# A masked softmax: the last 16 partitions of one batch stored through GpSimd's queue, and nine small reads after the last store

## The chip, the cores and the metric

The kernel runs on one core of a Trainium2 chip. That core has compute engines that run side by side, each with its own instruction stream: TensorE, VectorE, ScalarE, GpSimd and SyncE (here SyncE only issues transfers and waits). Sixteen DMA engines move data between the chip's memory (HBM) and the core's on-chip memory (SBUF), which has 128 partitions. A transfer issued by SyncE or ScalarE goes through a hardware queue of that engine; one issued by GpSimd goes through GpSimd's software queue. All queues are worked off by the same sixteen DMA engines. Order between the streams is kept with semaphores: a transfer adds to its semaphore when its data has landed (16 for a whole transfer), and an engine can wait until a semaphore has reached a number.

The metric is the device time of one launch in microseconds (us), as the median of several runs.

## The reference

The input `x` has the shape 16 x 8 x 256 x 256 (batch, heads, query, key) in float32, and every batch has one length between 128 and 255. For each row the softmax is taken over the first `length` keys; the rest of the row is zero.

```python
for b in range(batch):
    length = lengths[b]
    masked = x[b, :, :, :length].copy()
    masked = masked - np.max(masked, axis=-1, keepdims=True)
    exp_masked = np.exp(masked)
    result[b, :, :, :length] = exp_masked / np.sum(exp_masked, axis=-1, keepdims=True)
```

33.55 MB of output have to be written. Of the input, only the columns up to the length of the batch have to be read.

## The kernel before

One batch has 2,048 rows of 256 values. They lie on 128 partitions with 16 rows each (`nt` = 16, `half` = 8, `quarter` = 4), so one batch takes 16 KB of each partition, 2 MB in all. The tile `xt` has eight slots of one batch each; batch b is loaded into slot b % 8, changed in place, and stored from there.

**Loads.** SyncE issues the loads of batches 0 to 3 at full width (lines 107 to 111). From batch 4 on, GpSimd issues them in a loop (lines 153 to 160): it reads the length, waits until the store that freed the slot has landed, and picks one of twelve widths (160, 168, ... 240, 256 columns), so that it reads little more than is needed. The columns from 160 on of slots 4 to 7 have been set to zero before (line 149).

**Compute.** For each batch VectorE first pushes all columns past the length to a very negative number (`mask`, line 204, with `clip`, line 192). ScalarE then takes the exponential row by row and the sum of each row with it (lines 246 to 254, one semaphore count of `s_exp` per half batch). VectorE takes the reciprocal of the sums and multiplies (`divide`, line 216); each half batch adds one to `s_out`. The loop of lines 231 to 240 places the mask of the next batch among the two divides of this one; for batch 14 the mask of batch 15 comes first, then the two divides of 14, then the two of 15.

**Stores.** SyncE's stream, after its five load issues, is a plain list of stores (lines 114 to 122). `parts(b)` cuts a batch: batch 0 and batch 13 are stored whole, batches 1 to 7 in a half and two quarters, the others in two halves. Each store waits for its count of `s_out` (line 117); the first one of a batch also waits until the stores of the batch two before have landed (line 119, semaphores `s_st[0]` and `s_st[1]` for even and odd batches). Every store covers all 128 partitions:

```python
nc.sync.dma_start(
    out=out_f[b, :, s, :], in_=xt[:, b % slots, s, :]
).then_inc(s_b, 16 * ((s.stop - s.start) // quarter))
```

The order of the transfers in a queue is thus the order of the issues in the program. At the end SyncE waits until the stores of batches 14 and 15 have landed (lines 257 to 259), and the program closes.

Of the kernel before, what the change touches and what calls it, by code (L numbers as in the profile page):

```python
# [9 lines left out]
F32 = mybir.dt.float32  # L10
# [10 lines left out]
def kernel(  # L21
# [6 lines left out]
    nc = tc.nc  # L28
    P = nc.NUM_PARTITIONS

    batch, heads, seq_q, seq_k = x.shape
# [3 lines left out]
    half = nt // 2  # L35
    quarter = nt // 4

    x_f = x.rearrange("b h q k -> b (h q) k").rearrange("b (p t) k -> b p t k", p=P)
    out_f = out.rearrange("b h q k -> b (h q) k").rearrange("b (p t) k -> b p t k", p=P)

    slots = 8
# [2 lines left out]

    widths = list(range(160, 248, 8))
    low = widths[0]
    mid = seq_k // 2
    big = 1.0e30

    def parts(b):  # L50


        if b == 0:
            cuts = [0, nt]
        elif b < 8:
            cuts = [0, half, half + quarter, nt]
        elif b != batch - 3:
            cuts = [0, half, nt]
        else:
            cuts = [0, nt]  # L60
        return [slice(i, j) for i, j in zip(cuts, cuts[1:])]

    pool = ctx.enter_context(tc.tile_pool(name="all", bufs=1))
    psum = ctx.enter_context(tc.tile_pool(name="psum", bufs=1, space=bass.MemoryType.PSUM))
    xt = pool.tile([P, slots, nt, seq_k], F32, name="xt")
# [9 lines left out]
    inv_sum = pool.tile([P, batch, nt], F32, name="inv_sum")  # L75
    warm = pool.tile([P, 1], F32, name="warm")
    seed = pool.tile([1, 2], F32, name="seed")

    sem = lambda n: ctx.enter_context(nc.semaphore(n))
    s_st = [sem("s_st0"), sem("s_st1")]  # L80
    with tc.tile_critical(no_gpsimd_drain=True):  # L81
        s_word = sem("s_word")
        s_ones = sem("s_ones")
# [11 lines left out]
        s_out = sem("s_out")  # L95

        def length(engine, at):

            return nc.values_load(  # L99
                at,  # L100
                engines=[engine],
                skip_runtime_bounds_check_because="compared with constants, never an address",
            )


        nc.scalar.dma_start(out=word64, in_=lengths[None, :]).then_inc(s_word, 16)
        for h in range(2):
            s = slice(h * half, (h + 1) * half)
# [5 lines left out]
        for b in range(batch):  # L114
            s_b = s_st[b % 2]
            for s in parts(b):
                nc.sync.wait_ge(s_out, 2 * b + (s.stop - 1) // half + 1)
                if b >= 2 and s.start == 0:
                    nc.sync.wait_ge(s_b, 64 * (b // 2 + 1))
                nc.sync.dma_start(  # L120
                    out=out_f[b, :, s, :], in_=xt[:, b % slots, s, :]
                ).then_inc(s_b, 16 * ((s.stop - s.start) // quarter))

        def pick(v, n, slot, par, ws):

            if len(ws) == 1:
                w = ws[0]
                nc.gpsimd.dma_start(  # L130
                    out=xt[:, slot, :, :w], in_=x_n[:, n, :, :w]
                ).then_inc(s_sw[par], 16)
                return
            m = (len(ws) - 1) // 2
            with nc.gpsimd.If(v <= ws[m]):  # L135
                pick(v, n, slot, par, ws[: m + 1])
            with nc.gpsimd.Else():  # L137
                pick(v, n, slot, par, ws[m + 1 :])
# [14 lines left out]
        with nc.Fori(0, (batch - ahead) // 2, 1, engines=[POOL]) as q:  # L153
            for par in range(2):
                n = 2 * q + (ahead + par)
                v_len = length(POOL, word[0:1, bass.ds(2 * n, 1)])
                with nc.gpsimd.If(q >= 1):  # L157
                    nc.gpsimd.wait_ge(s_sw[par], 16 * q)
                    nc.gpsimd.wait_ge(s_st[par], 64 * q)  # L159
                pick(v_len, bass.ds(n, 1), bass.ds(n % slots, 1), par, widths + [seq_k])  # L160


        nc.tensor.wait_ge(s_ones, 1)
# [6 lines left out]
        def step(ins):  # L170
# [8 lines left out]
                out=down, in0=iota_i, scalar1=0.5, scalar2=-big, op0=ALU.add, op1=ALU.mult  # L179
# [7 lines left out]
                out=len_s, in0=len_f, scalar1=big, scalar2=None, op0=ALU.mult  # L187
# [58 lines left out]
        with nc.Fori(0, 2 * batch, 1, engines=[ACT]) as i:  # L246
            nc.scalar.wait_ge(s_min, i + 1)
            at = bass.ds(i % (2 * slots), 1)
            for j in range(half):
                e = x_h[:, at, j, :]  # L250
                ins = nc.scalar.activation(  # L251
                    out=e, in_=e, func=EXP, accum_out=sum_h[:, bass.ds(i, 1), j]
# [4 lines left out]
    with tc.tile_critical(no_gpsimd_drain=True):  # L257
        for par in range(2):
            nc.sync.wait_ge(s_st[par], 64 * (batch // 2 + 1))


# [28 lines left out]
```

The softmax here doesn't subtract the row's maximum and nothing guards it: scores larger than these inputs give would overflow.

## Time and profile before

| what | value |
|---|---|
| median of 9 runs | 156.3 us (155.81 to 156.71) |
| the profiled execution, its own time | 156.24 us |
| its span in the profile | 154.6 us |
| bytes moved | 62.08 MB (28.51 MB read from HBM, 33.55 MB written), 401 GB/s over the span |
| VectorE busy | 115.6 us, 75% of the span |
| ScalarE busy | 105.2 us, 68% |
| GpSimd busy | 19.0 us, 12% |
| VectorE's multiply on half a batch (line 222) | 32 times, 2292 ns each |
| GpSimd's issue of a load (line 130) | 12 times, 1064 ns each on average (558 to 1294) |
| SyncE's issue of a store (line 120) | 37 times, median 372 ns (341 to 1526) |

The span is what the profiler sees of the program; the launch's own time has 1.6 us more around it. The busy time of an engine is the sum of its instructions; waiting does not count. Lines L1, L2 and so on are lines of the kernel. "SPq" and "POOLq" are the instruction streams of SyncE and GpSimd in which they issue transfers. In the lines by window, five busy times (TensorE, its weight loads, VectorE, ScalarE, GpSimd), each with a count in brackets, are followed by TensorE's clock, the mean busy share of the sixteen DMA engines and the rate in GB/s. The packet records of the trace give the time of each piece that a DMA engine moves, without naming the engine; each transfer closes on each engine with a 4-byte record that counts its semaphore up.

### The profile page before, as it was taken

Reading aid. Unit: us, or ns where it says so; the run is one execution under the profiler, and the core shown is the slowest. Engines: PE = TensorE matmul, PEld = TensorE weight load, DVE = VectorE, ACT = ScalarE, POOL = GpSimd, SP = SyncE. Lnnn points to the kernel's source line nnn. Section 1 sums busy time; section 2 is a strip of 40 time slices with the busy share of each in tenths; the row PEclk is TensorE's granted clock in tenths of the full one; section 3 lists DMA queues with packets and bytes.
Section 4 is the critical chain, followed back from the end, with each engine's and each line's share of the span. In section 5 each row is a group of like instructions: output and inputs, shape, how many; then the busy total and the mean of one; then the engine's idle time right before and its main releaser. Section 6 shows DMA issues by size and latency. Waiting matters only on the chain.

```text
span 154.6 us, 1325 instructions
## 1 busy us (share of the span) xinstructions
PE 0.2 (0%) x1; PEld 0.1 (0%) x1; DVE 115.6 (75%) x84; ACT 105.2 (68%) x514; POOL 19.0 (12%) x25
## 2 busy tenths in 40 slices
PE   0000000000000000000000000000000000000000
PEld 0000000000000000000000000000000000000000
DVE  1249999952999696979979696969689683399700
ACT  3088799992592959778695959595975905979000
POOL 4910031000220110202011020202001000000000
DMA  4999999999999999999999999999999999999992
GB/s 110 432 441 420 445 386 402 406 404 445 402 410 388 412 410 417 411 415 411 411 424 404 419 409 406 415 418 417 413 426 414 413 451 420 426 443 411 428 424 102
DMA packets 10133, 62.08 MB, mean 401 GB/s; under 512 B 867, under 2 KB 963, under 8 KB 6291
## 3 DMA queue, kind: packets, MB, share of 16 engines
q1 hardware_dynamic: 6048, 41.95, 65.9%
q0 software_dynamic: 4080, 20.12, 32.1%
q14 instruction: 3, 0.02, 0.0%
q10 hardware_dynamic: 2, 0.00, 0.0%
HBM read 28.51 MB, written 33.55 MB: 401 GB/s over the span
## 4 chain that ended last, share of the span: by engine, by line
DMA 77%; DVE 8%; issue 5%; POOLq 3%; SPq 1%; POOL 0%; DVEq 0%
DMA xt<-in_x_dram 77%; DVE xt L222 6%; DVE xt L195 2%; POOLq L99 1%; POOLq L135 1%; POOLq L130 1%; SPq L109 1%; POOL xt L130 0%; DVE inv_sum L219 0%; SPq L111 0%; POOLq L157 0%; POOLq L153 0%; POOLq L159 0%; POOLq L137 0%; DVEq L212 0%
## 5 line engine op out<-in xcount | busy, mean ns | idle before, releaser
L251 ACT ACTIVATE xt<-xt x256 | 102.3, 401 | 36.3 <-DVE xt L195 36.3
L222 DVE TENSOR_TENSOR xt<-xt,inv_sum 128x2048 f32<-128x2048 f32 x32 | 73.3, 2292 | 1.1
L195 DVE SCALAR_TENSOR_TENSOR xt<-down,len_s,xt 128x2048 f32<-128x2048 f32 (+1 forms) x17 | 37.8, 2222 | 15.0 <-DMA xt<-in_x_dram 14.8
L251 ACT ACTIVATION_READ_ACCUMULATOR xt<-xt x256 | 47.8, 187 | 0.0
L130 POOL DMA_DIRECT2D xt<-in_x_dram x12 | 12.8, 1064 | 95.6 <-DMA out_dram<-xt 54.5
L219 DVE RECIPROCAL inv_sum<-row_sum 128x8 f32<-128x8 f32 x32 | 6.3, 198 | 12.1 <-ACT xt L251 12.1
L149 POOL MEMSET xt<- 128x1536 f32 x4 | 5.3, 1388 | 1.1 <-DVE len_s L186 1.1
L243 ACT ACT_TABLE_LOAD x1 | 1.3, 1283 | 1.6 <-SPq L81 1.6
L178 DVE TENSOR_SCALAR down<-iota_i 128x256 f32<-128x256 int32 x1 | 0.3, 297 | 1.6 <-POOL iota_i L141 1.6
L183 DVE CAST len_b<-word 1x16 bf16<-1x16 int32 x1 | 0.2, 162 | 0.4 <-DMA word<-in_lengths_dram 0.4
L186 DVE TENSOR_SCALAR len_s<-len_f 128x16 f32<-128x16 f32 x1 | 0.2, 174 | 0.3 <-PE len_f L165 0.3
L141 POOL IOTA iota_i<- 128x256 int32 x1 | 0.3, 332 | 0.6 <-SPq L81 0.6
L146 POOL MEMSET seed<- 1x1 f32 x2 | 0.3, 162 | 0.0
L243 ACT ACTIVATE warm<-const-float32-0.0 128x1 f32<-128x1 f32 x1 | 0.2, 203 | 0.0
L144 POOL MEMSET ones<- 1x128 bf16 x1 | 0.2, 194 | 0.0
L165 PE MATMUL len_f<-len_b,ones 1*128 1x16 bf16 x1 | 0.2, 165 | 2.6 <-DVE len_b L183 2.6
L274 POOL MEMSET const-float32-0.0<- 128x1 f32 x1 | 0.1, 99 | 0.3 <-issue 0.3
L165 PEld LDWEIGHTS len_f<-len_b,ones 1*128 1x128 bf16 x1 | 0.1, 100 | 2.6 <-POOL ones L144 2.6
L274 POOL MEMSET const-float32-1.0<- 128x1 f32 x1 | 0.1, 99 | 0.0
L274 POOL MEMSET const-bfloat16-1.0<- 128x1 bf16 x1 | 0.1, 99 | 0.0
L274 POOL MEMSET const-uint8-127<- 128x1 uint8 x1 | 0.1, 99 | 0.0
L274 POOL BASE_LOAD x1 | 0.0, 17 | 0.1
## 6 DMA issues: line engine op xcount, KB each, us to landing
out_dram<-xt SPq DMA_DIRECT2D x21, 1024.0 KB
out_dram<-xt SPq DMA_DIRECT2D x14, 512.0 KB
xt<-in_x_dram SPq DMA_DIRECT2D x3, 2048.0 KB, 16.2
xt<-in_x_dram POOLq DMA_DIRECT2D x3, 1728.0 KB, 16.9
out_dram<-xt SPq DMA_DIRECT2D x2, 2048.0 KB
xt<-in_x_dram POOLq DMA_DIRECT2D x2, 2048.0 KB, 18.3
xt<-in_x_dram POOLq DMA_DIRECT2D x2, 1600.0 KB, 17.0
xt<-in_x_dram POOLq DMA_DIRECT2D x2, 1280.0 KB, 14.9
```

The lines of the kernel that those rows point to most:

```text
L99: return nc.values_load(at, engines=[engine], skip_runtime_bounds_check_because="compared with constants, never an address",)
L109: nc.sync.dma_start(out=xt[:, 0, s], in_=x_f[0, :, s]).then_inc(s_ld[h], 16)
L130: nc.gpsimd.dma_start(out=xt[:, slot, :, :w], in_=x_n[:, n, :, :w]).then_inc(s_sw[par], 16)
L135: with nc.gpsimd.If(v <= ws[m]):
L149: nc.gpsimd.memset(xt[:, b, :, low:], 0.0).then_inc(s_fill, 1)
L165: nc.tensor.matmul(len_f, lhsT=ones, rhs=len_b, start=True, stop=True).then_inc(s_lenf, 1)
L195: return nc.vector.scalar_tensor_tensor(out=t, in0=down[:, None, lo:hi].to_broadcast([P, s.stop - s.start, hi - lo]), scalar=len_s[:, b : ...
L219: step(nc.vector.reciprocal(out=inv_sum[:, b, s], in_=row_sum[:, b, s]))
L222: nc.vector.tensor_tensor(out=t, in0=t, in1=inv_sum[:, b, s, None].to_broadcast([P, half, seq_k]), op=ALU.mult,).then_inc(s_out, 1)
L243: nc.scalar.activation(out=warm, in_=nc.const_aps.tensor(0.0, (P, 1), F32), func=EXP)
L251: ins = nc.scalar.activation(out=e, in_=e, func=EXP, accum_out=sum_h[:, bass.ds(i, 1), j])
L274: nc = _bacc.Bacc("TRN2", target_bir_lowering=False, num_devices=1)
```

## The change

Three things are changed.

1. The stores of batch 14 (`shared`) on SyncE cover partitions 0 to 111 only (`edge` = 112).
2. Partitions 112 to 127 of batch 14 are stored by GpSimd, behind its loop of loads. For each half it waits for the same count of `s_out` as SyncE's store does, and issues four transfers: for partitions 112 to 119 and then 120 to 127, one row of each partition (8 KB in all) and then the other seven (56 KB). `max_dma_last_dim` cuts the rows into pieces of 512 bytes. They count on a semaphore of their own, `s_edge`.
3. Behind its last store SyncE issues nine reads of a few columns of `x`, of 1, 2, 3, 4, 5, 6, 7, 8 and 12 partitions, 212 to 256 bytes of each, into a tile `spare` that nothing uses (`touch`). At the end SyncE waits for `s_edge` and `s_spare` as well.

```diff
+    shared = batch - 2
+    edge = P - 16
...
+    spare = pool.tile([16, 2, 9, 128], F32, name="spare")
...
+    s_edge = sem("s_edge")
+    s_spare = sem("s_spare")
+    probes = [1, 2, 3, 4, 5, 6, 7, 8, 12]
...
+        def touch(r):
+            for n, k in enumerate(probes):
+                w = 36 + 16 * r + k
+                nc.sync.dma_start(
+                    out=spare[:k, r, n, :w], in_=x_f[0, :k, 0, :w]
+                ).then_inc(s_spare, 16)
...
+                p = slice(0, edge if b == shared else P)
                 nc.sync.dma_start(
-                    out=out_f[b, :, s, :], in_=xt[:, b % slots, s, :]
+                    out=out_f[b, p, s, :], in_=xt[p, b % slots, s, :]
                 ).then_inc(s_b, 16 * ((s.stop - s.start) // quarter))
+        touch(1)
...
+        for h in range(2):
+            nc.gpsimd.wait_ge(s_out, 2 * shared + h + 1)
+            for p in (slice(edge, edge + 8), slice(edge + 8, P)):
+                for s in (slice(h * half, h * half + 1), slice(h * half + 1, (h + 1) * half)):
+                    nc.gpsimd.dma_start(
+                        out=out_f[shared, p, s, :],
+                        in_=xt[p, shared % slots, s, :],
+                        max_dma_last_dim=4 * mid,
+                    ).then_inc(s_edge, 16)
...
+        nc.sync.wait_ge(s_edge, 128)
+        nc.sync.wait_ge(s_spare, 16 * len(probes))
```

## The prediction

> **What bounds the kernel now.** I read the page's slices first, then the queues, then SyncE's own waits and issues, and last the busy shares of the final microseconds. The slices (part 2; each digit is the busy share of one fortieth of the span, 3.87 us):
>
> ```profile
> DVE  1249999952999696979979696969689683399700
> ACT  3088799992592959778695959595975905979000
> POOL 4910031000220110202011020202001000000000
> DMA  4999999999999999999999999999999999999992
> ```
>
> The 16 DMA engines are full from the second slice to the last but one; VectorE and ScalarE have gaps throughout. The kernel must move 62.08 MB, and at about 415 GB/s that is the span. So an edit counts through two things only: what the DMA engines do, and what follows their last byte. The queues (part 3) and SyncE's answers on waits and time:
>
> ```profile
> q1 hardware_dynamic: 6048, 41.95, 65.9%
> q0 software_dynamic: 4080, 20.12, 32.1%
> ...
> SPq L285 <- DMA out_dram<-xt: 6.2, 1, 6.2
> ...
> 115.28 31.23 SPq L120 DMA_DIRECT2D out_dram<-xt  x9
> ```
>
> Queue 1 is SyncE's (all stores), queue 0 is GpSimd's (loads from batch 4 on). SyncE has issued its last store at 115.28 + 31.23 = 146.51 us and then waits 6.2 us for stores. The chain of waits cannot be used for this end: it stops at VectorE's last multiply, 143.82 + 2.29 = 146.11 us, and 8.5 us follow it. The windows tell what happens in them (after the bracketed counts: clock, DMA busy share, GB/s):
>
> ```profile
> 146.15:151.00 4.85, 0.00 (x0) 0.00 (x0) 0.00 (x0) 0.00 (x0) 0.00 (x0) 1.00 1.02 429
> 151.00:151.50 0.50, 0.00 (x0) 0.00 (x0) 0.00 (x0) 0.00 (x0) 0.00 (x0) 1.00 0.82 344
> 151.50:152.00 0.50, 0.00 (x0) 0.00 (x0) 0.00 (x0) 0.00 (x0) 0.00 (x0) 1.00 0.36 148
> 152.00:152.50 0.50, 0.00 (x0) 0.00 (x0) 0.00 (x0) 0.00 (x0) 0.00 (x0) 1.00 0.16 66
> 152.50:153.00 0.50, 0.00 (x0) 0.00 (x0) 0.00 (x0) 0.00 (x0) 0.00 (x0) 1.00 0.04 16
> ```
>
> 429 GB/s over 16 engines is 26.8 GB/s each: 8 KB in 0.31 us. A share of 0.16 is 0.16 x 16 = 2.6 engines: about three engines finish late. The packet records say the same: the 16 completion records of the last store run from 151.20 to 152.89 us, the thirteenth is at 152.02, the last three at 152.59, 152.73 and 152.89. Work left after 151.0 is 0.5 x (0.82 + 0.36 + 0.16 + 0.04) = 0.69 us per engine; spread evenly it would end at 151.7. So perfect balance is worth 1.2 us, and no more. The last semaphore count arrives at 153.37, the span ends at 154.6, the execution's own time is 156.24.
>
> [...]
>
> **The change, part by part.**
>
> *Removed.* Both stores of batch 14 on SyncE lose partitions 112–127: 16 x 16 KB = 256 KB, 16 KB per engine, 16,384 / 26.8 = 0.61 us less for each.
>
> *Added on GpSimd.* Eight transfers. [...] Issue: no row shows so small a transfer from GpSimd; its loads took 0.56 to 1.29 us each, 1.06 on average. First half: from 138.80 (end of VectorE's multiply for batch 14), four by 143.0; second half by 147.3[...], ahead of 151.2, where the first engine runs dry. This is hidden unless one issue takes over 1.5 us (138.8 + 8 x 1.5 = 150.8). Behind GpSimd's new waits stands only its own end; its last load was issued at 116.2, and nothing refills the slot of batch 14.
>
> [...]
>
> *The 112-partition stores.* [...] With engines up to 1.7 us out of step I take 0.3 in all. [...]
>
> *The nine reads.* SyncE's store issues have a median of 372 ns: 146.51 + 9 x 0.37 = 149.9, before 151.2, so the issue hides behind the queued stores. [...] The 128-byte read of the lengths took 11 + 9 ns in the packet records[...]. [...] If SyncE's queue blocked behind the stores the issue would follow them, +2 to 3 us; five loads of 8 MB were issued by 3.7 us, so I see no such block. [...] I take 0.1 in all.
>
> VectorE and ScalarE keep their order and their work. Sum: +1.8 + 0.3 + 0.1 = +2.2 us. Against its own time 156.24 that is 158.4; the median is 156.3, so the same figure stands against it, 1.3% slower.
>
> **Rivals.** *Balance works (ends below before).* Place: the three late engines. [...] 0.4 us saved, 155.8, or 155.9 with the reads. For it: three engines clearly are late. [...] *Bytes only[...].* [...] 156.8 to 157.1. [...] *Nothing to see.* The pieces land evenly[...] and the reads are hidden: 156.2 to 156.5. For it: DMA bytes are unchanged in sum.
>
> **How the numbers follow.** Forecast[...]: 0.48, its own range 157.2 to 161.0. Bytes only: 0.25. Nothing to see: 0.13. Balance: 0.14. A difference under 0.2% (0.3 us) can't be told from none here. Slower 0.48 + 0.25 = 0.73, same 0.13, faster 0.14. The range from 155.7 to 161.0 takes in the balance case[...]; what lies above (crowding in the 112-partition stores) and below I put at 2 in 10.
>
> **What would show it.** [...] in the windows from 139 to 149 us the DMA engines stay busy but move fewer GB/s (429 before), and the store wait on the last line of SyncE grows from 6.2 to about 8 us. Bytes only: full rate, a tail of few engines longer by half a microsecond. Balance: shares after 151.5 that fall from near 1 to 0 within half a microsecond. Reads: SyncE's last issue near 150, one engine's completions at the end; if the issue ends after 152, it blocked. Issues on GpSimd over 1.5 us each would make it the bound. The forecast is wrong if the rate stays at 429 GB/s with the 112-partition stores in flight: then only bytes and late engines decide.

## The result, and the profile after

The changed kernel takes 159.12 us (median of 10 runs, 158.19 to 162.53); the kernel before 156.2 us (31 runs, 155.81 to 156.71). The ratio is 1.0195, 95% interval 1.0174 to 1.0215: 3.0 us slower (a difference in us is here the ratio applied to the time of before). Ratios here are taken over undisturbed executions only; where stores of 112 partitions themselves spread the times, median and range of all runs are given beside the ratio.

The profiled execution has a time of 159.14 us and a span of 157.5 us, 2.9 more than before. The rates by slice of the kernel before, then the slices of the changed kernel:

```profile
GB/s 110 432 441 420 445 386 402 406 404 445 402 410 388 412 410 417 411 415 411 411 424 404 419 409 406 415 418 417 413 426 414 413 451 420 426 443 411 428 424 102
```

```profile
DMA  4999999999999999999999999999999999999980
GB/s 112 431 435 437 424 387 409 409 406 450 407 402 402 394 416 416 411 421 403 413 411 413 420 401 423 411 419 417 412 421 418 425 439 416 441 422 360 340 365 13
```

Up to the 36th slice the rates are like those of before. Then the engines stay busy but move 360, 340 and 365 GB/s, where before has 411, 428 and 424. The same place in windows, first of the kernel before, then of the changed one (last two columns: DMA busy share, GB/s):

```profile
144.00:146.50 2.50, 0.00 (x0) 0.00 (x0) 2.12 (x1) 0.00 (x0) 0.00 (x0) 1.00 1.03 436
146.50:149.00 2.50, 0.00 (x0) 0.00 (x0) 0.00 (x0) 0.00 (x0) 0.00 (x0) 1.00 1.00 423
```

```profile
144.00:146.50 2.50, 0.00 (x0) 0.00 (x0) 2.47 (x3) 0.01 (x1) 0.70 (x2) 1.00 1.02 330
146.50:149.00 2.50, 0.00 (x0) 0.00 (x0) 0.53 (x1) 0.00 (x0) 0.00 (x0) 1.00 0.95 314
...
152.00:153.00 1.00, 0.00 (x0) 0.00 (x0) 0.00 (x0) 0.00 (x0) 0.00 (x0) 1.00 0.83 345
153.00:154.00 1.00, 0.00 (x0) 0.00 (x0) 0.00 (x0) 0.00 (x0) 0.00 (x0) 1.00 0.29 117
154.00:155.00 1.00, 0.00 (x0) 0.00 (x0) 0.00 (x0) 0.00 (x0) 0.00 (x0) 1.00 0.05 8
```

Over the 5 us from 144 to 149, 2.5 x (436 - 330) + 2.5 x (423 - 314) = 538 KB less are moved, 1.25 us of the full rate. The packet records say which packets: before, an 8 KB store packet takes 309 ns, and of the 512 after 140.5 us only one takes over 330. In the changed kernel 53 of 480 do, up to 1,008 ns, 10.3 us more than 309 each in sum; the edge, whose rows the program cuts into pieces of 512 bytes, stands in the records as packets of 4 KB, 3 KB and 1 KB, 32 of each, and they take 6.8 us more than their shortest (159, 121 and 46 ns). Together 17.1 us, 1.07 us for each of 16 engines.

The end, in SyncE's issues and waits of the changed kernel:

```profile
114.53 32.90 SPq L135 DMA_DIRECT2D out_dram<-xt  x9
147.49 6.71 SPq L115 DMA_DIRECT2D spare<-in_x_dram  x9
...
SPq L316 <- DMA spare<-in_x_dram: 0.9, 1, 0.9
```

SyncE no longer waits for a store at the end, as it did for 6.2 us before, but for the reads. The semaphore counts divide the 2.9 us: the stores' last count comes at 154.54 (153.37 before), +1.17; the reads' last at 155.72, another +1.18; and from the last count to the end of the span pass 1.80 us (1.26 before), +0.54.

### The profile page after: what moved, and what is told of

Same layout as the page of the kernel before. It is cut to its first block, busy times and chain, and to the rows that moved or that the text cites. A ratio compares the mean times of both kernels' runs of the same rounds, so it can differ in the third digit from the quotient of the medians.

```text
span 157.5 us, 1343 instructions
## 1 busy us (share of the span) xinstructions
PE 0.2 (0%) x1; PEld 0.1 (0%) x1; DVE 115.7 (73%) x84; ACT 105.2 (67%) x514; POOL 23.7 (15%) x33
## 4 chain that ended last, share of the span: by engine, by line
DMA 66%; DVE 19%; issue 4%; SPq 1%; ACT 1%; POOLq 1%; ACTq 0%; DVEq 0%
DMA xt<-in_x_dram 45%; DMA out_dram<-xt 21%; DVE xt L251 12%; DVE xt L224 6%; ACT xt L280 1%; DVE inv_sum L248 1%; SPq L135 1%; SPq L123 1%; ACTq L280 0%; POOLq L146 0%; SPq L125 0%; POOLq L151 0%; DVEq L241 0%; POOLq L173 0%; POOLq L153 0%
## 5 line engine op out<-in xcount | busy, mean ns | idle before, releaser
L185 POOL DMA_DIRECT2D out_dram<-xt x8 | 4.6, 582 | 22.4 <-DVE xt L251 22.3
## 6 DMA issues: line engine op xcount, KB each, us to landing
xt<-in_x_dram POOLq DMA_DIRECT2D x2, 1600.0 KB, 17.1
```

Of the source, the lines that this page charges most:

```text
L185: nc.gpsimd.dma_start(out=out_f[shared, p, s, :], in_=xt[p, shared % slots, s, :], max_dma_last_dim=4 * mid,).then_inc(s_edge, 16)
```

## The experiments

All times are against the kernel before on the same chip (medians 156.0 to 156.3 us); each kernel has 4 to 20 executions behind its median, the two single ones named below apart. The theory had two costs that add up: the stores of batch 14 slow the DMA engines when they go by partitions, and the reads prolong the end. The rivals were that the reads alone do it, that GpSimd's queue does, or that the reads only follow late stores.

**The edge alone, then the reads alone.** The first kernel is the changed one without its reads:

```diff
-        touch(1)
...
-        nc.sync.wait_ge(s_spare, 16 * len(probes))
```

> The edge through GpSimd and the 112-partition stores, without the nine reads. Theory A (two costs that add: [...], and the reads prolong the end): +1.2 us over the kernel before, about 157.5 us, with the rate falling to 310 to 340 GB/s between 144 and 149 us. Theory B (the reads alone make the time; the edge costs nothing of its own): 156.2 us within 0.3. Theory C (the reads are innocent, the stores end late and the reads only follow): 158.8 us or more.

158.04 us, ratio 1.0108 (1.0076 to 1.0140): +1.7 us. Its windows:

```profile
144.00:146.50 2.50, 0.00 (x0) 0.00 (x0) 2.00 (x1) 0.00 (x0) 0.00 (x0) 1.00 1.01 349
146.50:149.00 2.50, 0.00 (x0) 0.00 (x0) 0.00 (x0) 0.00 (x0) 0.00 (x0) 1.00 1.01 338
```

The rate falls without any read. The second keeps the reads and stores batch 14 as before, without GpSimd's loop and the wait for `s_edge`:

```diff
-                p = slice(0, edge if b == shared else P)
+                p = slice(0, P)
```

> The nine small reads behind the last store, with all stores at 128 partitions on SyncE as before. Theory A: SyncE issues each read in about 1.0 us while stores are in flight and in 0.3 us after, so the last read lands about 1.2 to 1.6 us after the last store: +1.2 to +1.8 us, 157.4 to 158.0 us, and the store's last completion stays at 152.9. Theory B: +2.9 us, 159.1. Theory C: within 0.3 us of before.

157.6 us, ratio 1.0084 (1.0062 to 1.0107): +1.3 us. The two losses add up, 1.7 + 1.3 = 3.0, to the whole, within their intervals (1.2 to 2.2, and 1.0 to 1.7). Rivals B (reads alone) and C (reads innocent) fall. The stores' last count is at 153.39 us, as before; the reads' last at 154.39, a whole microsecond later, although SyncE had issued them early. Their issue, by the view of that line (shortest, median, longest ns; first and last start):

```profile
L115 SPq DMA_DIRECT2D spare<-in_x_dram x9: 269/296/1054, 147.5 to 151.4; - x9
```

So a long issue (1.05 us) of the kind that I had named in the expectation is there, but it is not what ends this run: the last issue is over at 151.74 us. The last five counts are 154.03, 154.13, 154.21, 154.32 and 154.39. The counts don't name engines, but this is what two engines taking turns would give, with 0.18 to 0.19 us on each from read to read. By the packet records the two engines that finished their stores last had six and five reads still to do, which makes the microsecond.

**The same bytes through GpSimd, over all 128 partitions.** No reads; GpSimd stores the last row of each half in all partitions, SyncE the other seven rows:

```diff
-                p = slice(0, edge if b == shared else P)
+                t = slice(s.start, s.stop - 1 if b == shared else s.stop)
...
-            for p in (slice(edge, edge + 8), slice(edge + 8, P)):
-                for s in (slice(h * half, h * half + 1), slice(h * half + 1, (h + 1) * half)):
+            s = slice((h + 1) * half - 1, (h + 1) * half)
...
-                        out=out_f[shared, p, s, :],
-                        in_=xt[p, shared % slots, s, :],
+                out=out_f[shared, :, s, :],
+                in_=xt[:, shared % slots, s, :],
```

> The same 256 KB of batch 14 go through GpSimd's queue in the same pieces of 512 bytes, but as the last row of each half in all 128 partitions[...]; SyncE stores the other seven rows of all 128 partitions; no reads. [...] no loss, 156.2 us within 0.3, rate near 429 GB/s throughout. Rival (GpSimd's queue, its small pieces or its descriptors slow the engines[...]): a loss like that of the edge alone, +0.8 to +1.2 us.

156.21 us, ratio 1.0002 (0.9989 to 1.0015). Windows:

```profile
144.00:146.50 2.50, 0.00 (x0) 0.00 (x0) 2.06 (x1) 0.00 (x0) 0.00 (x0) 1.00 1.02 424
146.50:149.00 2.50, 0.00 (x0) 0.00 (x0) 0.00 (x0) 0.00 (x0) 0.00 (x0) 1.00 1.03 431
```

256 KB of batch 14 through GpSimd's queue (4,176 packets there, 4,080 before) cost nothing. It is the choice of partitions that costs, not the queue. (Whether the changed kernel also shares the edge out unevenly among the engines, no trace tells: the packets name no engine.)

**Half the partitions at a time.** The kernel before, with each store of batch 14 cut at partition 64:

```diff
+                if b == batch - 2:
+                    for p in (slice(0, P // 2), slice(P // 2, P)):
+                        nc.sync.dma_start(
+                            out=out_f[b, p, s, :], in_=xt[p, b % slots, s, :]
+                        ).then_inc(s_b, 16)
+                    continue
```

> Only the kernel before with each store of batch 14 cut into partitions 0 to 63 and 64 to 127, both on SyncE; same bytes, same queue, no reads. [...] 2 MB go at half the rate (about 215 GB/s instead of 429): up to 4.9 us more, at least 2, 158.3 to 161 us. Rival[...]: two more issues of 0.37 us each that hide behind queued stores, 156.2 us within 0.3.

158.92 us, ratio 1.0159 (1.0121 to 1.0198): +2.5 us, from nothing but a cut by partitions.

```profile
144.00:146.50 2.50, 0.00 (x0) 0.00 (x0) 1.86 (x1) 0.00 (x0) 0.00 (x0) 1.00 0.99 302
146.50:149.00 2.50, 0.00 (x0) 0.00 (x0) 0.00 (x0) 0.00 (x0) 0.00 (x0) 1.00 0.99 272
```

The rate falls to 272 GB/s, not to 215, and 136 of its 512 packets take over 330 ns. Of these, 37 take between 600 and 640 ns, about twice 309. The loss is about half of the 4.9 us expected at most; the half rate behind that figure was my estimate. What makes the packets slow is not shown: a cut by partitions changes which addresses of HBM are written at the same time as well as which partitions are read, and no run separates the two.

**The 112-partition stores alone.** From the kernel with the edge alone, GpSimd's part is taken out as well (partitions 112 to 127 of batch 14 are not stored at all, and there are no reads):

```diff
-        for h in range(2):
-            nc.gpsimd.wait_ge(s_out, 2 * shared + h + 1)
...
-        nc.sync.wait_ge(s_edge, 128)
```

> Only the two 112-partition stores; partitions 112 to 127 of batch 14 are not stored at all, and there are no reads. [...] the missing 16 KB per engine save 0.6 us: 155.6 us. [...] about 156.5 us, and 8 KB packets above 600 ns appear. [...]

The 156.5 us rested on an estimate of how much packets would be slowed, from no run. The 20 runs go from 155.22 to 159.56 us with a median of 156.74; the ratio (1.0009, 0.9986 to 1.0033) covers only part of that spread, and the spread is what matters here (the kernel before stays within 155.78 and 156.48 us in its 41 executions beside it). Two more executions were profiled:

> The kernel with the 112-partition stores alone once more (partitions 112 to 127 of batch 14 are not stored), for one more look, since its times spread from 155.2 to 159.6 us and the one profiled was the fastest. [...] the slower this execution, the more time its 8 KB packets after 141 us take over their usual 309 ns (3.3 us in sum in the profile of 155.22), about 16 us in sum, one per engine, for each microsecond of time. If something else makes it (a late load, the end): packets stay at 309 ns whatever the time.

> The same kernel a third time, for the same reason and with the same expectation.

Times of the three profiled executions: 155.22, 156.26 and 160.68 us. Time that the 8 KB packets took over 309 ns: 3.3, 5.0 and 10.6 us in sum. The order is as expected, though three executions are few; the proportion is not: 16 us of slowed packets per microsecond of time were foreseen, 7.3 / 5.5 = 1.3 us were found. The windows of the slowest show why:

```profile
149.00:151.00 2.00, 0.00 (x0) 0.00 (x0) 0.00 (x0) 0.00 (x0) 0.00 (x0) 1.00 1.02 406
151.00:153.00 2.00, 0.00 (x0) 0.00 (x0) 0.00 (x0) 0.00 (x0) 0.00 (x0) 1.00 0.27 98
153.00:155.00 2.00, 0.00 (x0) 0.00 (x0) 0.00 (x0) 0.00 (x0) 0.00 (x0) 1.00 0.10 41
155.00:157.50 2.50, 0.00 (x0) 0.00 (x0) 0.00 (x0) 0.00 (x0) 0.00 (x0) 1.00 0.06 26
```

A share of 0.06 is one engine of sixteen. From 155 us until its stores end at 157.5 us one engine alone works; the others are done. When the packets are linked by their start and end times, ten slow ones between 142.7 and 152.3 us stand in this engine's chain, and together they take 5.4 us over 309 ns each: half of the 10.6 us lies on one engine. The slow packets don't spread evenly, and the end waits for the engine that has most of them.

**The edge on SyncE's queue**, as one store of 16 partitions per half behind the 112-partition store; GpSimd's part is out:

```diff
+                if b == shared:
+                    nc.sync.dma_start(
+                        out=out_f[b, edge:, s, :], in_=xt[edge:, b % slots, s, :]
+                    ).then_inc(s_edge, 16)
```

> The 112-partition stores, and the edge as one store of 16 partitions per half on SyncE's own queue, in rows of 8 KB; GpSimd's queue is not used for it[...]; no reads. [...] +1 to +2.5 us, 157.2 to 158.7 us. Rival (GpSimd's queue[...] make the loss): 156.2 us within 0.3.

156.94 us (156.26 to 158.69, 14 runs), ratio 1.0061 (1.0041 to 1.0080): +1.0 us.

```profile
144.00:146.50 2.50, 0.00 (x0) 0.00 (x0) 2.47 (x3) 0.14 (x2) 0.00 (x0) 1.00 0.98 380
146.50:149.00 2.50, 0.00 (x0) 0.00 (x0) 0.65 (x1) 0.00 (x0) 0.00 (x0) 1.00 1.02 380
```

A loss without GpSimd, at the low end of what was expected. The 112-partition stores are in it as well, so this does not weigh the edge by itself.

**Small pieces of neighbouring partitions, without 112-partition stores.** The row edge again, 16 partitions at a time:

```diff
+            for k in range(0, P, 16):
                 nc.gpsimd.dma_start(
-                    out=out_f[shared, :, s, :],
-                    in_=xt[:, shared % slots, s, :],
+                    out=out_f[shared, k : k + 16, s, :],
+                    in_=xt[k : k + 16, shared % slots, s, :],
```

> As the run with the row edge (last row of each half through GpSimd, all SyncE stores on 128 partitions, no reads), but GpSimd stores it 16 neighbouring partitions at a time, eight transfers per half in place of one. [...] +0.4 to +1.5 expected, 156.6 to 157.6 us. Rival (only the 112-partition stores cost, or small pieces pass between other packets unnoticed): 156.2 us within 0.3.

156.93 us, ratio 1.0043 (1.0027 to 1.0060): +0.7 us, inside the first range expected, but the packets don't make it. The 1 KB packets took 46 ns in the median and only 1.4 us in sum over that, 0.08 us per engine, and the windows show 404 and 423 GB/s. The stores' last count is at 153.54. What is late is GpSimd's last piece: it issues sixteen at 0.5 us until 148.1, and their last count comes at 153.73, 0.36 us after the last count of before. Another 0.37 us fall behind it: GpSimd's closing instruction (DRAIN), 488 ns long in the kernel before, takes 6,978 ns here, until 154.6 us, and SyncE waits for it. These two make the 0.7 us:

```profile
L314 POOLq DRAIN x3: 40/84/6978, 147.7 to 155.1; - x3
```

That 1 KB packets slow each other is not shown.

**The reads: more partitions, another queue, fewer.** Nine reads of 16 partitions:

```diff
-    probes = [1, 2, 3, 4, 5, 6, 7, 8, 12]
+    probes = [16] * 9
```

> Nine reads of 16 partitions each (208 to 272 bytes wide) behind the last store in place of those of 1 to 12; stores as before. Theory (reads queue on each engine and complete one after the other, about 0.17 us each, as six reads took 1.0 us on the latest engine of the run with the reads alone): [...] the latest ends 9 x 0.17 = 1.5 us after its stores, +1.9 us with the 0.4 us of closing, 158.1 us. Rival (what costs is the issue of a read that uses fewer than 16 engines, 1.0 us each at worst): issues of 0.37 us, all done by 151, and the time within 0.5 us of before.

158.36 us, ratio 1.0145 (1.0118 to 1.0172): +2.3 us. Reads of 16 partitions cost more, so it isn't that a read has few. But SyncE issued its last store only at 147.9 us in this execution (146.1 before), the issues took 420 ns in the median (two took over 1.0 us), and the last one ended at 153.7, after the stores: here issue and reads both count, and the run does not separate them.

The nine reads of the change, issued by ScalarE behind its last exponential:

```diff
-                nc.sync.dma_start(
+                nc.scalar.dma_start(
                     out=spare[:k, r, n, :w], in_=x_f[0, :k, 0, :w]
...
             ins.then_inc(s_exp, 1)
+
+        touch(1)
```

> The same nine reads, issued by ScalarE behind its last exponential (about 143 us), so that they pass through another queue while the last stores are still queued; SyncE waits for them at the end as before. If what costs is that the reads stand behind the last store: 156.2 us within 0.3, or up to 156.7 if the 0.4 us between SyncE's last waits stays. If reads cost the engines anything while stores run: +1 us or more.

156.12 us, ratio 1.0002 (0.9991 to 1.0013). The reads are issued from 141.4 us on, and their last count is at 150.85, while the stores run until 153.30. SyncE's last waits, in order, are for the reads, then for the stores:

```profile
SPq L305 <- DMA spare<-in_x_dram: 3.2, 1, 3.2
SPq L305 <- DMA out_dram<-xt: 2.4, 1, 2.4
```

As work for the engines the reads cost nothing that can be measured here; they cost where they stand behind the last store. One read of 12 partitions in that place:

```diff
-    probes = [1, 2, 3, 4, 5, 6, 7, 8, 12]
+    probes = [12]
```

> Only the last of the nine reads (12 partitions) behind the last store, all stores as before. Theory (each read adds about 0.17 us on an engine, and a fixed 0.4 us falls between SyncE's last waits when it waits for reads of its own queue): +0.2 to +0.6 us, 156.4 to 156.8 us. Rival (the cost of the reads is fixed, whatever their number): +1.3 us, 157.5 us.

156.66 us, ratio 1.0030 (1.0020 to 1.0040): +0.5 us. In the profiled execution, which took 157.12 us, the read's last count comes 0.19 us after the stores'. The cost grows with the number, so it is not fixed.

## Why the prediction was right, and where it was not

**The bound.** Right: DMA engines busy to the end, 62.1 MB, and an end made of the last bytes and of what follows them. The first rival, balance, had 155.8 us and rested on where the three late engines are; the packet records name no engine, so that was not shown. The time decides: a loss where it had a gain. What the records do show is how many packets a read makes: SyncE's queue has 96 more with the reads alone than before (6,144 against 6,048), a read and a completion for each of 1 + 2 + ... + 8 + 12 = 48 partitions.

**The stores of batch 14.** Right that they slow the DMA engines: the same bytes cost nothing with stores over 128 partitions (ratio 1.0002), and a pure cut at partition 64 cost 2.5 us, with 302 and 272 GB/s where before has 436 and 423. Why an engine is slower there, no trace shows, and the +1.8 us for the edge and +0.3 us for the 112-partition stores were my estimates, which no trace showed. That an engine takes turns between its two queues is seen in the trace of before: of the 681 data packets that start between 70 and 78 us, 511 can be linked by their times to one next packet alone, and for 501 of these the next is of the other queue: mostly one of a load (4,416 bytes) and one of a store (8,192 or 4,096 bytes) in turn.

The sum predicted for edge and 112-partition stores was 1.8 + 0.3 = +2.1 us; measured +1.7 (interval 1.2 to 2.2). The two terms were divided wrongly, though. I put the 112-partition stores at +0.3. Alone they have a median of 156.74 us against 156.07, +0.7, although they move 16 KB per engine less, worth 0.6: some +1.3. I had taken it small because the engines are up to 1.7 us out of step (152.89 - 151.20). But the end is set by the engine that has most slow packets, and in the slowest execution one gathered 5.4 us over 309 ns each. If the two parts add, the edge then has about +1.0 left (1.7 - 0.7), where I had 2.4 before subtracting the bytes (1.8 + 0.6); its pieces were slowed by 3.7 us in sum in the run with the edge alone, 0.23 us for each of 16 engines if spread evenly. This division is rough: with the ratio of the 112-partition stores (1.0009, +0.1 us) in place of the medians they cost 0.7 before the saved bytes are taken off and the edge 1.6. Either way the stores cost more than I had put, and the edge less.

On which engines the loss lies was not shown. In the changed kernel's profile the last store packet ends at 154.21 us; another ends at 154.00 us, and right behind it stand packets of the reads of 2, 3, 4, 5 and 6 partitions, which start between 154.00 and 154.08 us.

**Which packets slow each other** was not shown either. After 140.5 us 8 KB packets do get slower (53 of 480 over 330 ns in the changed kernel, one of 512 before), but the records name neither their partitions nor their engines.

**GpSimd's issue.** Hidden, as said: eight issues of 542 to 635 ns, cheaper than the 1.06 us taken, over at 144.7 us. The first packet of the edge starts only at 143.7, 3.7 us after its issue began, yet the last count of the edge (150.26) is well ahead of the stores' (154.54).

**The reads.** This step failed: +0.1 us predicted, +1.3 measured. I priced a read at its packet and its completion, 0.02 us on an engine. The counts of reads on one engine follow each other at 0.17 to 0.19 us. With the reads alone this makes the whole microsecond, since all reads are issued before the stores end. In the changed kernel, the count of the store that ends at 154.00 comes at 154.35, and eight counts of reads follow it at steps of 0.17 us, from 154.52 to 155.72; by their times they are those of one engine, and the last three, 155.38, 155.55 and 155.72, end all counts. But there the issue was late as well: it ended at 154.20 us where I had 149.9, and by the sign that I had named (later than 152) it was held up. The packets of the ninth read start only at 154.81 to 154.93, and all counts but those last three are in by 155.27. No run parts the two in that kernel. In both kernels a late engine had reads behind its stores. A further 0.4 us fell between two of SyncE's last waits with nine reads on its own queue (in the changed kernel and with the reads alone) and not with one read or with ScalarE's (0.2 us); its cause stays open.

**The sum.** Predicted +2.2 us (158.4), measured +3.0 (159.12, in the forecast's own range): edge and 112-partition stores 0.4 too much, reads 1.2 too little. The range did not need the two errors to offset each other: the edge alone, at 158.04 us, lies in it. Of the signs named in advance the fall of the rate came, from 144 us on (from 139 to 144 it is much as before). SyncE's store wait did not grow to 8 us in the changed kernel, because the reads' wait took its place; with the edge alone it is 8.0 us, in two waits.

## What to carry to other kernels

In a kernel whose DMA engines are full to the end, a transfer over other partitions than all 128 is not just fewer bytes: here a cut at partition 64 cost 2.5 us. Split by rows instead, which cost nothing here (ratio 1.0002). Price slow packets on the engine that gets most of them (5.4 of 10.6 us on one, in one execution), not on the mean. Keep anything, however tiny, from standing behind the last store in its queue, or issue it early enough, on another queue, that stores still cover it (nine reads cost 1.3 us behind the last store, and nothing measurable from ScalarE's queue).

## What the runs showed that I had not expected

- The counts of small reads come one after the other on a DMA engine, 0.17 to 0.19 us apart, while their packet records last 14 to 18 ns.
- Issuing a small read took SyncE between 0.27 and 1.05 us. With the reads alone six of nine took about 0.3 us and one 1.05 us; in the changed kernel the first five took 1.00 to 1.05 us and the last four 0.30, by the view of that line:

```profile
L115 SPq DMA_DIRECT2D spare<-in_x_dram x9: 295/1000/1051, 147.5 to 153.9; - x9
```

The long issues came early, while stores were still outstanding, but no run isolates the cause.

- Stores of 112 partitions alone spread the times of one kernel over 5.5 us (155.22 to 160.68), where the kernel before stays within 0.9 us (155.81 to 156.71).
